# Tanh-gated double matmul on one core: transposing x on the DMA crossbar, 512-column matmuls over mixed w1|w2 banks, and a head run slice by slice

## The chip, the cores and the metric

One NeuronCore of one Trainium2 chip. The metric is the device time of one execution in microseconds, as the median of several runs. The profiler's record of one execution gives the span and the trace that the text reads.

## The reference

```python
# x: (16, 512, 1024) float32; w1, w2: (1024, 768) float32
y1 = np.matmul(x, w1)
y2 = np.matmul(x, w2)
return (np.tanh(y1) * y2).astype(np.float32)
```

## The kernel before

The 16 x 512 rows of x are 64 row tiles of 128 rows (`mt`). The 1024 values of k are 8 slices of 128 (`ko`); the 768 output columns are two halves of 384 (`nt`). Products run on TensorE in bf16 and are summed in float32 in PSUM.

The weights come first: two DMAs on SP's queue (L48, L49) load w1 and w2 whole, 3 MB each, as float32, and one cast each (L52, L53) makes the bf16 copies `w1_b` and `w2_b`. The framework puts the first cast on DVE and the second on ACT, since `nc.any` leaves the engine open.

Then one loop over the 64 row tiles. A DMA on POOL's queue loads a row tile and casts it to bf16 on the way (`x_b`, L63, four buffers). TensorE needs the slice with k on the partitions, so each of the eight 128x128 blocks is transposed by a matmul with an identity into PSUM (`pt`, L67, four banks), and copied to `xT` in SBUF by ACT or DVE (L68). For each half, sixteen matmuls of 384 columns follow, taking turns between the bank of w1 (`ps1`, L77) and the bank of w2 (`ps2`, L79); both have two buffers. ACT takes the tanh of `ps1` into `t1` (L82), DVE multiplies it with `ps2` into `o` (L84), and SP stores the half (L85).

Every matmul is preceded on TensorE by the load of its stationary operand (the 128x128 block of `xT`), which the trace shows as PEld. Each engine works its instructions off in order; the framework's scheduler sets that order and the waits. In `[waits ...]` below, DMASW and DMAHW are completions of DMAs issued from POOL and from SP, eight counters of each in turn, and PE, DVE and Activation are completions on these engines.

Of the kernel before, what the change touches and what calls it, by code (L numbers as in the profile page):

```python
# [1 line left out]

# [5 lines left out]


@with_exitstack
def kernel(
    ctx: ExitStack,
    tc: tile.TileContext,
    x: bass.AP,
    w1: bass.AP,
    w2: bass.AP,
    out: bass.AP,
):
    nc = tc.nc  # L20
    P = 128
    B, M, K = x.shape
    K2, N = w1.shape
    assert K == K2
    BM = B * M
    assert BM % P == 0 and K % P == 0
    KO = K // P
    MT = BM // P
    N_TILE = 384
    assert N % N_TILE == 0  # L30
    NT = N // N_TILE

    xf = x.flatten_outer_dims().rearrange("(mt p) k -> mt p k", p=P)
    of = out.flatten_outer_dims().rearrange("(mt p) n -> mt p n", p=P)
    w1r = w1.rearrange("(ko ki) n -> ki ko n", ki=P)
    w2r = w2.rearrange("(ko ki) n -> ki ko n", ki=P)

    bf16 = mybir.dt.bfloat16
    f32 = mybir.dt.float32

    const = ctx.enter_context(tc.tile_pool(name="const", bufs=1))
    ident = const.tile([P, P], bf16)
    make_identity(nc, ident)

    wpool = ctx.enter_context(tc.tile_pool(name="wpool", bufs=1))
    w1_f = wpool.tile([P, KO, N], f32)
    w2_f = wpool.tile([P, KO, N], f32)
    nc.sync.dma_start(w1_f, w1r)  # L48
    nc.sync.dma_start(w2_f, w2r)  # L49
    w1_b = wpool.tile([P, KO, N], bf16)  # L50
    w2_b = wpool.tile([P, KO, N], bf16)
    nc.any.tensor_copy(w1_b, w1_f)  # L52
    nc.any.tensor_copy(w2_b, w2_f)  # L53

    xpool = ctx.enter_context(tc.tile_pool(name="xpool", bufs=4))
    xtpool = ctx.enter_context(tc.tile_pool(name="xtpool", bufs=4))
    tppool = ctx.enter_context(tc.tile_pool(name="tp_psum", bufs=4, space=bass.MemoryType.PSUM))
    mmpool = ctx.enter_context(tc.tile_pool(name="mm_psum", bufs=2, space=bass.MemoryType.PSUM))
    opool = ctx.enter_context(tc.tile_pool(name="opool", bufs=4))

    for mt in range(MT):
        x_b = xpool.tile([P, K], bf16, tag="x_b")
        nc.gpsimd.dma_start(x_b, xf[mt])  # L63
        xT = xtpool.tile([P, KO, P], bf16)
        for ko in range(KO):
            pt = tppool.tile([P, P], bf16, tag="tp")
            nc.tensor.transpose(pt, x_b[:, ko * P:(ko + 1) * P], ident)  # L67
            nc.any.tensor_copy(xT[:, ko, :], pt)  # L68

        for nt in range(NT):  # L70
            ns = nt * N_TILE
            ps1 = mmpool.tile([P, N_TILE], f32, tag="ps1")
            ps2 = mmpool.tile([P, N_TILE], f32, tag="ps2")
            for ko in range(KO):
                st = ko == 0
                sp = ko == KO - 1
                nc.tensor.matmul(ps1, xT[:, ko, :], w1_b[:, ko, ns:ns + N_TILE],  # L77
                                 start=st, stop=sp)
                nc.tensor.matmul(ps2, xT[:, ko, :], w2_b[:, ko, ns:ns + N_TILE],  # L79
                                 start=st, stop=sp)  # L80
            t1 = opool.tile([P, N_TILE], f32, tag="t1")
            nc.scalar.activation(t1, ps1, mybir.ActivationFunctionType.Tanh)  # L82
            o = opool.tile([P, N_TILE], f32, tag="o")
            nc.vector.tensor_tensor(o, t1, ps2, mybir.AluOpType.mult)  # L84
            nc.sync.dma_start(of[mt, :, ns:ns + N_TILE], o)  # L85


# [1 line left out]
_INS = ['x', 'w1', 'w2']  # L89
_OUTS = [((16, 512, 768), 'float32')]  # L90


# [23 lines left out]
```

## Time and profile before

| | us |
|---|---|
| median of 3 runs | 414.83 |
| lowest, highest | 414.63, 414.93 |
| span of the profiled execution | 413.0 |
| TensorE busy with matmuls in it | 381.2 |
| ACT, DVE, POOL busy | 128.7, 107.2, 36.8 |

The span runs from the first instruction to the last. The time of a run is taken around the execution and is a little longer than the span. The profiled execution has no time of its own outside the profiler, so the median stands beside its span. Busy time of matmuls counts each record to its modelled end, which lies after the start of the next one; what one matmul costs in a stream is therefore read from the step between starts. The page of the profile gives, below the busy times, DMA queues (packets, megabytes, the time that their packets took as a share of the time of 16 engines), the chain of work that ended last, and groups of instructions as `line engine op out<-in xcount | busy, mean ns of one | idle time before them, and who ended it`.

### The profile page before, as it was taken

What the parts mean: (1) busy time and instruction counts of PE and PEld (TensorE: products, weight loads), DVE (VectorE), ACT (ScalarE), POOL (GpSimd) and SP (SyncE); (2) the same over time, 40 slices, a digit from 0 to 9 for tenths busy, and PEclk for the clock granted to TensorE, in tenths of its full rate; (3) what the DMA queues carried; (4) which work ended last, traced back from release to release, by engine and by line L of the source; (5) the groups of instructions that cost most, each with busy time, mean ns of one, the idle gap of its engine ahead of it and who ended that gap; (6) DMA issues with size and microseconds to landing.
All of it is one profiled execution on the core that took longest, in us unless ns stands there. A gap on an engine that the chain in (4) does not pass through costs nothing.

```text
span 413.0 us, 6572 instructions
## 1 busy us (share of the span) xinstructions
PE 381.2 (92%) x2560; PEld 235.9 (57%) x2560; DVE 107.2 (26%) x316; ACT 128.7 (31%) x455; POOL 36.8 (9%) x70
## 2 busy tenths in 40 slices
PE   1496999999999999999999999999999999999995
PEld 0253666666666666666666666666666666666663
DVE  0301232232223232222323232232223232222322
ACT  1434132332333233323323332332333233323322
POOL 2400001110110011011101101110110011011000
PEclk9998999999999999999999999999999999999999
DMA  8971345444444543444354345434444543444221
GB/s 255 294 264 40 101 123 119 107 108 116 110 109 101 129 109 104 110 108 117 95 128 108 106 106 120 111 102 116 109 110 102 128 106 106 108 110 116 71 77 58
DMA packets 29760, 48.67 MB, mean 118 GB/s; under 512 B 3104, under 2 KB 19488, under 8 KB 29728
## 3 DMA queue, kind: packets, MB, share of 16 engines
q0 software_dynamic: 9216, 16.78, 24.7%
q1 hardware_dynamic: 20512, 31.47, 21.1%
q8 instruction: 20, 0.33, 0.3%
q14 instruction: 12, 0.10, 0.1%
HBM read 39.85 MB, written 25.17 MB: 157 GB/s over the span
## 4 chain that ended last, share of the span: by engine, by line
PE 86%; DMA 7%; DVE 3%; ACT 1%; issue 1%; SPq 0%
PE ps L79 41%; PE ps L77 38%; PE pt L67 7%; DMA w_f<-in_w_dram 7%; DVE xT L68 3%; ACT w_b L53 1%; DVE o L84 0%; ACT t L82 0%; SPq L48 0%
## 5 line engine op out<-in xcount | busy, mean ns | idle before, releaser
L79 PE MATMUL ps<-w_b,xT 128*128 128x384 bf16 x1024 | 326.7, 328 | 4.2 <-ACT w_b L53 4.2
L77 PE MATMUL ps<-w_b,xT 128*128 128x384 bf16 x1024 | 327.0, 328 | 1.6 <-DVE w_b L52 1.6
L82 ACT ACTIVATE t<-ps 128x384 f32<-128x384 f32 x128 | 62.7, 490 | 266.8 <-PE ps L77 263.3
L77 PEld LDWEIGHTS <-xT 128*128 128x128 bf16 x1024 | 100.6, 98 | 77.4 <-issue 19.7
L79 PEld LDWEIGHTS <-xT 128*128 128x128 bf16 x1024 | 100.5, 98 | 67.9 <-issue 6.0
L84 DVE TENSOR_TENSOR o<-t,ps 128x384 f32<-128x384 f32 x128 | 70.9, 554 | 179.7 <-ACT t L82 158.5
L67 PE MATMUL pt<-ident,x_b 128*128 128x128 bf16 x512 | 64.0, 223 | 21.5 <-DMA x_b<-in_x_dram 12.5
L68 ACT COPY xT<-pt 128x128 bf16<-128x128 bf16 x325 | 65.6, 271 | 11.7 <-PE pt L67 11.1
L63 POOL DMA_DIRECT2D x_b<-in_x_dram x64 | 36.2, 566 | 342.9 <-PE pt L67 342.5
L68 DVE COPY xT<-pt 128x128 bf16<-128x128 bf16 x187 | 36.0, 221 | 117.5 <-PE pt L67 114.7
L67 PEld LDWEIGHTS <-x_b 128*128 128x128 bf16 x512 | 39.7, 99 | 26.9 <-DMA x_b<-in_x_dram 13.9
L53 ACT CAST w_b<-w_f 128x6144 bf16<-128x6144 f32 x1 | 5.3, 5312 | 1.0 <-DMA w_f<-in_w_dram 1.0
L52 DVE CAST w_b<-w_f 128x6144 bf16<-128x6144 f32 x1 | 3.4, 3361 | 5.1 <-DMA w_f<-in_w_dram 5.1
L68 ACT ACT_TABLE_LOAD x1 | 1.3, 1283 | 0.7 <-PEq L100 0.7
masks.py:199 POOL TENSOR_SCALAR_AFFINE_SELECT ident<-ident 128x128 bf16<-128x128 bf16 x1 | 0.3, 304 | 0.1
masks.py:197 POOL MEMSET ident<- 128x128 bf16 x1 | 0.2, 204 | 0.3 <-POOLq L100 0.3
L100 POOL MEMSET const-float32-0.0<- 128x1 f32 x1 | 0.1, 98 | 0.2 <-issue 0.2
L100 POOL MEMSET const-bfloat16-1.0<- 128x1 bf16 x1 | 0.1, 102 | 0.0
L100 POOL MEMSET const-uint8-127<- 128x1 uint8 x1 | 0.1, 102 | 0.0
L100 POOL MEMSET const-float32-1.0<- 128x1 f32 x1 | 0.1, 98 | 0.0
## 6 DMA issues: line engine op xcount, KB each, us to landing
out_dram<-o SPq DMA_DIRECT2D x128, 192.0 KB, 1.9
x_b<-in_x_dram POOLq DMA_DIRECT2D x64, 256.0 KB, 3.7
w_f<-in_w_dram SPq DMA_DIRECT2D x2, 3072.0 KB, 22.0
```

What stands on the lines that cost most here:

```text
L52: nc.any.tensor_copy(w1_b, w1_f)
L53: nc.any.tensor_copy(w2_b, w2_f)
L63: nc.gpsimd.dma_start(x_b, xf[mt])
L67: nc.tensor.transpose(pt, x_b[:, ko * P:(ko + 1) * P], ident)
L68: nc.any.tensor_copy(xT[:, ko, :], pt)
L77: nc.tensor.matmul(ps1, xT[:, ko, :], w1_b[:, ko, ns:ns + N_TILE], start=st, stop=sp)
L79: nc.tensor.matmul(ps2, xT[:, ko, :], w2_b[:, ko, ns:ns + N_TILE], start=st, stop=sp)
L82: nc.scalar.activation(t1, ps1, mybir.ActivationFunctionType.Tanh)
L84: nc.vector.tensor_tensor(o, t1, ps2, mybir.AluOpType.mult)
L100: nc = _bacc.Bacc("TRN2", target_bir_lowering=False, num_devices=1)
```

## The change

- x is still loaded and cast by POOL's queue (`load_x`), into eight buffers. A DMA on SP's queue, `dma_start_transpose`, then writes `xT` from `x_b`, in SBUF, in place of eight transposes on TensorE and eight copies. The identity is gone.
- The weights are no longer loaded whole and cast by an engine. POOL's queue loads them with cast in slices of one k each (`load_w`), into eight tiles `w_b[k]` that hold, for each of three chunks of 256 columns, 256 of w1 beside 256 of w2. The slices of the first two chunks come first, with the loads of the first four row tiles between them, then the slices of the third chunk.
- One matmul covers a whole chunk: 512 columns, w1 and w2 in one PSUM bank (`mm`). All eight banks are one ring (`bank`). The tanh reads the left half of a bank, the product the right half (`finish`), 256 columns each. A row tile is stored by one DMA of 768 columns (`store`).
- The first four row tiles are run with k as the outer loop over their first two chunks, in eight banks; their third chunk follows, row tile by row tile. From the fifth row tile on, the loop runs row tile by row tile, three chunks of eight matmuls each, with `load_x` called four row tiles ahead.
- `pin` keeps every instruction in the order of the code on its engine.

```diff
-    w1_f = wpool.tile([P, KO, N], f32)
-    w2_f = wpool.tile([P, KO, N], f32)
-    nc.sync.dma_start(w1_f, w1r)
-    nc.sync.dma_start(w2_f, w2r)
-    nc.any.tensor_copy(w1_b, w1_f)
-    nc.any.tensor_copy(w2_b, w2_f)
-        for ko in range(KO):
-            pt = tppool.tile([P, P], bf16, tag="tp")
-            nc.tensor.transpose(pt, x_b[:, ko * P:(ko + 1) * P], ident)
-            nc.any.tensor_copy(xT[:, ko, :], pt)
...
+    HALF = 256
+    NC = N // HALF
+    HEAD = 4
+    AHEAD = 4
...
+    xpool = ctx.enter_context(tc.tile_pool(name="xpool", bufs=HEAD + AHEAD))
+    xtpool = ctx.enter_context(tc.tile_pool(name="xtpool", bufs=HEAD + AHEAD))
+    pspool = ctx.enter_context(tc.tile_pool(name="ps", bufs=8, space=bass.MemoryType.PSUM))
+    tpool = ctx.enter_context(tc.tile_pool(name="tpool", bufs=4))
     opool = ctx.enter_context(tc.tile_pool(name="opool", bufs=4))
+    w_b = [wpool.tile([P, NC, 2, HALF], bf16, name=f"w_b{k}") for k in range(KO)]
+    def load_w(k, c0, c1):
+        for h, src in ((0, w1r), (1, w2r)):
+            pin(nc.gpsimd.dma_start(
+                w_b[k][:, c0:c1, h, :],
+                src[:, k, c0 * HALF:c1 * HALF].rearrange("p (c j) -> p c j", j=HALF)))
+    def load_x(mt):
+        x_b = xpool.tile([P, K], bf16, tag="x_b", name="x_b")
+        pin(nc.gpsimd.dma_start(x_b, xf[mt]))
+        xT = xtpool.tile([P, KO, P], bf16, tag="xT", name="xT")
+        pin(nc.sync.dma_start_transpose(xT, x_b))
+        xts[mt] = xT
+    def finish(mt, c, ps, o):
+        t1 = tpool.tile([P, HALF], f32, tag="t1", name="t1")
+        pin(nc.scalar.activation(t1, ps[:, :HALF], ACT.Tanh))
+        pin(nc.vector.tensor_tensor(o[:, c * HALF:(c + 1) * HALF], t1, ps[:, HALF:], ALU.mult))
+    def mm(ps, mt, k, c):
+        pin(nc.tensor.matmul(ps, xts[mt][:, k, :], w_b[k][:, c, :, :].rearrange("p h j -> p (h j)"),
+                             start=k == 0, stop=k == KO - 1))
...
+    for k in range(3, KO):
+        load_w(k, 0, 2)
+    for k in range(KO):
+        load_w(k, 2, NC)
+    for mt in range(HEAD, HEAD + AHEAD):
+        load_x(mt)
+    head = {(mt, c): bank() for mt in range(HEAD) for c in range(2)}
+    for k in range(KO):
+        for mt in range(HEAD):
+            for c in range(2):
+                mm(head[mt, c], mt, k, c)
...
+    for mt in range(HEAD, MT):
+        if mt + AHEAD < MT:
+            load_x(mt + AHEAD)
+        o = new_o()
+        for c in range(NC):
+            ps = bank()
+            for k in range(KO):
+                mm(ps, mt, k, c)
+            finish(mt, c, ps, o)
+        store(mt, o)
```

The order of instructions at three places. First POOL, from the start of the program, before: the loads of x alone, with the identity between them.

```order
masks.py:197 MEMSET ident 128x128
L63 DMA x_b<-in_x_dram 128x1024
masks.py:199 ISA
masks.py:199 AFFINE_SELECT ident<-ident 128x128
L63 DMA x_b<-in_x_dram 128x1024 x63
```

POOL after, from its first DMA; the slices of two chunks are `128x2x256`.

```order
L63 DMA x_b<-in_x_dram 128x1024
L57 DMA w_b_73<-in_w_dram 128x2x256 x2
L63 DMA x_b<-in_x_dram 128x1024
L57 DMA w_b_74<-in_w_dram 128x2x256 x2
L63 DMA x_b<-in_x_dram 128x1024
L57 DMA w_b_75<-in_w_dram 128x2x256 x2
L63 DMA x_b<-in_x_dram 128x1024
L57 DMA w_b_76<-in_w_dram 128x2x256 x2
```

The weights have moved from SP's queue to POOL's, and the fourth row tile's load stands behind six weight slices. Sixteen slices of the first part, sixteen of the second and sixty loads of x make up the rest of the row.

Second, SP's queue, before, with waits: the weights, then one store after another, each waiting for DVE.

```order
L48 DMA w_f<-in_w_dram 128x8x768
L49 DMA w_f<-in_w_dram 128x8x768
L85 DMA out_dram<-o 128x384 [waits DVE_49] x6
L85 DMA out_dram<-o 128x384 [waits DMAHW0_49,DVE_49]
L85 DMA out_dram<-o 128x384 [waits DMAHW1_49,DVE_49]
```

SP's queue after, from the transposes of the seventh and eighth row tile to the tenth's.

```order
L65 DMA_TRANSPOSE xT<-x_b 128x8x128 [waits DMASW6_49]
L65 DMA_TRANSPOSE xT<-x_b 128x8x128 [waits DMASW7_49]
L77 DMA out_dram<-o 128x768 [waits DMAHW0_49,DVE_49]
L77 DMA out_dram<-o 128x768 [waits DMAHW1_49,DVE_49]
L77 DMA out_dram<-o 128x768 [waits DMAHW2_49,DVE_49]
L77 DMA out_dram<-o 128x768 [waits DMAHW3_49,DVE_49]
L65 DMA_TRANSPOSE xT<-x_b 128x8x128 [waits DMAHW4_49,DMASW0_49,PE_49]
L77 DMA out_dram<-o 128x768 [waits DMAHW5_49,DVE_49]
L65 DMA_TRANSPOSE xT<-x_b 128x8x128 [waits DMAHW6_49,DMASW1_49,PE_49]
```

Transposes and stores now share the queue: a transpose waits for its x_b, and every store stands behind the transpose ahead of it and the other way round.

Third, TensorE after, from its first matmul, which waits for the first weight slice (DMASW1); the numbers are those of buffers.

```order
L80 MATMUL ps_145<-w_b0_73,xT_83 128x512 [waits DMASW1_49]
L80 LDWEIGHTS xT_83
L80 MATMUL ps_146<-w_b0_73,xT_83 128x512
L80 LDWEIGHTS xT_89 [waits DMAHW1_49]
L80 MATMUL ps_147<-w_b0_73,xT_89 128x512
L80 LDWEIGHTS xT_89
L80 MATMUL ps_148<-w_b0_73,xT_89 128x512
L80 LDWEIGHTS xT_95 [waits DMAHW2_49]
L80 MATMUL ps_149<-w_b0_73,xT_95 128x512
L80 LDWEIGHTS xT_95
L80 MATMUL ps_150<-w_b0_73,xT_95 128x512
L80 LDWEIGHTS xT_101 [waits DMAHW3_49]
```

The first slice of k is run for all four row tiles before the second slice, so the fourth row tile's transpose (DMAHW3) stands ahead of all that follows. Before, TensorE's first work was the transposes of the row tiles that had been loaded, and its first product waited for the cast of a whole weight.

More of the change, by code (lines that the diff above doesn't have):

```diff
@@ L5 @@
 import concourse.tile as tile
-from concourse import bass_utils, mybir
+from concourse import mybir
 from concourse._compat import with_exitstack
-from concourse.masks import make_identity
+ACT = mybir.ActivationFunctionType
+ALU = mybir.AluOpType
 @with_exitstack
@@ L22 @@
     B, M, K = x.shape
-    K2, N = w1.shape
-    assert K == K2
+    _, N = w1.shape
     BM = B * M
-    assert BM % P == 0 and K % P == 0
     KO = K // P
     MT = BM // P
-    N_TILE = 384
-    assert N % N_TILE == 0
-    NT = N // N_TILE
+    HALF = 256
+    NC = N // HALF
+    HEAD = 4
+    AHEAD = 4
+    bf16 = mybir.dt.bfloat16
+    f32 = mybir.dt.float32
     xf = x.flatten_outer_dims().rearrange("(mt p) k -> mt p k", p=P)
@@ L36 @@
     w2r = w2.rearrange("(ko ki) n -> ki ko n", ki=P)
[L38 to L43, printed above, removed]
-    wpool = ctx.enter_context(tc.tile_pool(name="wpool", bufs=1))
-    w1_f = wpool.tile([P, KO, N], f32)
-    w2_f = wpool.tile([P, KO, N], f32)
-    nc.sync.dma_start(w1_f, w1r)
-    nc.sync.dma_start(w2_f, w2r)
-    w1_b = wpool.tile([P, KO, N], bf16)
@@ L51 @@
[L51 to L58, printed above, removed]
-    opool = ctx.enter_context(tc.tile_pool(name="opool", bufs=4))
@@ L61 @@
[L61 to L64, printed above, removed]
-        for ko in range(KO):
-            pt = tppool.tile([P, P], bf16, tag="tp")
[L67 to L85, printed above, removed]
@@ new lines, in finish, with new_o, store @@
+    def finish(mt, c, ps, o):
+        t1 = tpool.tile([P, HALF], f32, tag="t1", name="t1")
+        pin(nc.scalar.activation(t1, ps[:, :HALF], ACT.Tanh))
+        pin(nc.vector.tensor_tensor(o[:, c * HALF:(c + 1) * HALF], t1, ps[:, HALF:], ALU.mult))
+    def new_o():
+        return opool.tile([P, N], f32, tag="o", name="o")
+    def store(mt, o):
+        pin(nc.sync.dma_start(of[mt], o))
+    def mm(ps, mt, k, c):
+        pin(nc.tensor.matmul(ps, xts[mt][:, k, :], w_b[k][:, c, :, :].rearrange("p h j -> p (h j)"),
+                             start=k == 0, stop=k == KO - 1))
@@ new lines, in bank @@
+    def bank():
+        return pspool.tile([P, 2 * HALF], f32, tag="ps", name="ps")
+    load_x(0)
+    load_w(0, 0, 2)
+    load_x(1)
+    load_w(1, 0, 2)
+    load_x(2)
+    load_w(2, 0, 2)
+    load_x(3)
+    for k in range(3, KO):
[9 more added lines that the diff above has]
+                mm(head[mt, c], mt, k, c)
@@ new lines @@
+    outs = [new_o() for _ in range(HEAD)]
+    for mt in range(HEAD):
+        for c in range(2):
+            finish(mt, c, head[mt, c], outs[mt])
+    for mt in range(HEAD):
+        ps = bank()
+        for k in range(KO):
+            mm(ps, mt, k, 2)
+        finish(mt, 2, ps, outs[mt])
+        store(mt, outs[mt])
+    for mt in range(HEAD, MT):
[3 more added lines that the diff above has]
+        for c in range(NC):
+            ps = bank()
+            for k in range(KO):
+                mm(ps, mt, k, c)
+            finish(mt, c, ps, o)
+        store(mt, o)
```

2 lines of the change are left out of this document (added).

## The prediction

> **What bounds the kernel now.** First the head of the page and the chain of waits, to see which engine carries the end; then the timeline of the first 44 us and of one row tile in the middle; last the queues and groups, for prices.
>
> ```profile
> span 413.0 us, 6572 instructions
> PE 381.2 (92%) x2560; PEld 235.9 (57%) x2560; DVE 107.2 (26%) x316; ACT 128.7 (31%) x455; POOL 36.8 (9%) x70
> by line: PE ps L79 40.7%; PE ps L77 38.4%; PE pt L67 7.1%; DMA w_f<-in_w_dram 6.7%; DVE xT L68 3.4%; ACT w_b L53 1.3%; issue 1.0%; DVE o L84 0.1%; ACT t L82 0.1%; SPq L48 0.1%
> 1.24 27.87 DMA w_f<-in_w_dram
> 29.13 5.32 ACT w_b L53
> 34.49 9.64 PE ps L79 x48
> ```
>
> TensorE, busy 92%, carries the end. The chain has two parts that are not product: the transposes with the copies behind them (7.1% + 3.4% of 413.0 = 43.4 us), and a head of 34.5 us in which w2 is loaded whole and cast whole.
>
> ```profile
> 20.31 9.92 PE L77 MATMUL ps<-w_b,xT 128*128 128x384 bf16 x48 [1.64 <-DVE w_b L52]
> 103.68 0.32 PE L77 MATMUL ps<-w_b,xT 128*128 128x384 bf16 x1
> ...
> 108.39 0.33 PE L79 MATMUL ps<-w_b,xT 128*128 128x384 bf16 x1
> 108.55 0.75 PE L67 MATMUL pt<-ident,x_b 128*128 128x128 bf16 x5
> 403.25 0.21 PE pt L67 x3
> 34.50:44.00 9.50, 9.50 (x49) 5.29 (x49) 2.77 (x5) 1.66 (x6) 0.00 (x0) 0.82 0.23 85
> 120.00:240.00 120.00, 117.05 (x803) 73.06 (x801) 32.72 (x100) 37.82 (x140) 10.55 (x20) 1.00 0.46 111
> ```
>
> In the head only 48 of the 2048 matmuls run before 34.49. In the middle, 103.68 to 108.39 are 29 steps of one 384-column matmul: 4.71 / 29 = 0.1624 us each. The last column but two of the windows is the granted clock: 1.00 in the middle, 0.82 from 34.5 to 44, just after TensorE stood still. The next figure, 0.46, is the share of the DMA engines.
>
> **The matmuls.** 2048 of 384 columns become 64 x 3 x 8 = 1536 of 512, the same columns in all. The price of 512 isn't in the trace. In proportion to columns it is 0.1624 x 512/384 = 0.2166 us. The three 128-column transposes (0.21 us, 0.07 each) give the other end: a straight line from 0.07 at 128 through 0.1624 at 384 reaches 0.2086. I take 0.2166, since 384 is nearer to 512 and the transposes are another kind of matmul. The other end is 1530 x 0.008 = 12 us less. (The Trainium skill, TensorE: Matmul & The Clock Gate, Part 1, gives 215.7 ns from start to start for 512 columns at full clock; the sum by it is 1.4 us lower.) The weight load of each (98 ns, below) fits under 0.2166, as it did under 0.1624. The mixed w1|w2 bank costs TensorE nothing: the operand is still 512 columns in a row.
>
> **Transposes, copies, casts and identity: removed.** Of ACT's and DVE's copies only the 3.4% in the chain was path; the rest lay beside matmuls. Tanh and product go from 2 x 384 to 3 x 256 columns.
>
> ```profile
> L82 ACT ACTIVATE t<-ps 128x384 f32<-128x384 f32 x128 | 62.7, 490 | 266.8 <-PE ps L77 263.3
> L79 PEld LDWEIGHTS <-xT 128*128 128x128 bf16 x1024 | 100.5, 98 | 67.9 <-issue 6.0
> L84 DVE TENSOR_TENSOR o<-t,ps 128x384 f32<-128x384 f32 x128 | 70.9, 554 | 179.7 <-ACT t L82 158.5
> L63 POOL DMA_DIRECT2D x_b<-in_x_dram x64 | 36.2, 566 | 342.9 <-PE pt L67 342.5
> ```
>
> A 256-column tanh lies between 327 ns (in proportion) and 490, a product between 369 and 554. Even at the upper ends a row tile asks 3 x 0.49 = 1.5 us of ACT and 1.7 of DVE in its 24 x 0.2166 = 5.20 us, with eight banks in the ring: hidden.
>
> **The crossbar.** Each row tile issues one more DMA, on SP, in front of a store.
>
> ```profile
> q0 software_dynamic: 9216, 16.78, 24.7%
> q1 hardware_dynamic: 20512, 31.47, 21.1%
> HBM read 39.85 MB, written 25.17 MB: 157 GB/s over the span
> out_dram<-o SPq DMA_DIRECT2D x128, 192.0 KB, 1.9
> x_b<-in_x_dram POOLq DMA_DIRECT2D x64, 256.0 KB, 3.7
> L85 SPq DMA_DIRECT2D out_dram<-o x128: 332/332/360, 37.9 to 409.5; - x128
> ```
>
> One load of x takes 0.247 x 413.0 / 64 = 1.59 us of all 16 engines. The hardware queue takes 0.211 x 413.0 = 87.1 us for 31.47 MB, of which 25.17 is output: 69.7 us, 1.09 per row tile. Together 2.68 of the coming 5.20, so a transpose may take 2.5 us of the engines before they fill. No crossbar row exists. Its 256 KB at the rate of the hardware queue (44 ps per byte per engine) are 0.73 us. If instead each of its 1024 pieces of 256 B costs a whole packet of that queue (87.1 x 16 / 20512 = 68 ns), it is 4.35 us. I take 0.73: packets here are paid by the byte. Of the HBM read, 33.55 MB is x as float32, so a load's packet moves 33.55 MB / 9216 = 3.6 KB, 2.4 times the 1.5 KB of the hardware queue's, and costs 0.247 x 413.0 x 16 / 9216 = 177 ns, 2.6 times. Both ends stay for the range. SP's issue isn't shown either: a store's 0.33, or, were each of the eight blocks issued by itself, 2.7, which with the store still fits 5.20; I take 0.33. Latency: 0.33 to issue, 1.9 to land as a store does, 0.73: 3.0 us from x_b to xT. In the steady part a row tile is transposed about four tiles, 20 us, ahead of its use, and POOL runs ahead of SP, so 3 us is covered. The store queued behind a transpose waits at most that long; four output buffers give it 20 us. If the transpose outgrew 2.5 us that cover would drain, tile by tile, and xT would be what TensorE waits for.
>
> **The head.** Whole loads and casts give way to 32 slice loads with cast on POOL's queue, with x between them.
>
> ```profile
> 1.27 0.66 POOL L63 DMA_DIRECT2D x_b<-in_x_dram  x1 [0.32 <-issue]
> 2.26 1.62 POOL L63 DMA_DIRECT2D x_b<-in_x_dram  x3
> 17.62 2.76 POOL L63 DMA_DIRECT2D x_b<-in_x_dram  x1 [1.87 <-PE pt L67]
> L63 POOL DMA_DIRECT2D x_b<-in_x_dram x64: 527/527/2760, 1.3 to 379.8; - x64
> 408.17 0.33 PE L79 MATMUL ps<-w_b,xT 128*128 128x384 bf16 x1
> 409.47 0.33 SPq L85 DMA_DIRECT2D out_dram<-o  x1
> ```
>
> A load of x is 128 runs and 0.53 us of POOL. A first-part slice (two chunks) is 256 runs: between 0.53 and twice that, 1.05, which I take; a second-part slice is 128 runs, 0.53. With the identity gone POOL starts at about 0.9. Ahead of x3 stand three loads of x and six slices: 0.9 + 1.6 + 6.3 = 8.8; landed 3.7 later, 12.5 (by the engines' time, 4 x 1.59 + 6 x 0.80 = 11.2 us of loads, it could be 1 to 2 us later); transposed 15.5. TensorE starts at 0.9 + 3.7 + 3.0 = 7.6 with tile 0 but, in order, can't pass the fourth tile's first slice before 15.5, having done 6 matmuls. The last first-part slice is issued by 9.3 + 10 x 1.05 = 19.8 and lands at 23.5, ahead of its use near 28. From 15.5 come 58 matmuls (12.6) and a cold start: the two stretches of 48 matmuls took 9.92 and 9.64 where 48 x 0.1624 = 7.8, so 1.8 to 2.1 lost; 2.0 here. That is 30.1. The second-part slices are issued by 28.3 and land by 32.0; the first row tile needs the last of them at 31.6, a stall of 0.4. Its bank is free: the first of the eight is finished 7 matmuls (1.5 us) before the last, and tanh plus product take 1.05 at most. The 32 matmuls end at 37.4; x4 is issued at 28.3, landed at 32.0, transposed at 35.0, in time.
>
> **The sum.** 15.5 to pass x3, 2.0 cold, 1530 x 0.2166 = 331.4, stall 0.4, and the end: last matmul done at 408.3 of 413.0, so 4.7 from there through tanh, product and store (the smaller tanh and product save at most 0.35, the larger store gives that back). Together 354.0 of span. The runs' median, 414.83, stands 1.83 over the profiled span: 355.8, so 356.
>
> **Rivals.**
>
> (a) The crossbar becomes the bound, the one that ends slower. At 4.35 us per row tile the DMA engines need 1.59 + 1.09 + 4.35 = 7.03, against 5.20 on TensorE. Head 37.4, 8.7 later since four transposes of 4.35 stand in line before x3 is through (4.6 + 2.2 + 17.4 = 24.2), 60 x 7.03 = 422, end 4.7: 473 of span, 475. At 177 ns a piece it is 11.3 us, and beyond 850. It decides from 37.4 + 60t + 4.7 = 413, t = 6.18, a transpose of 3.5 us, or 55 ns a piece. For it: nothing in the trace moves pieces this small, and all 1024 must pass. Against: packets here cost by bytes, 11 ns for 256 B. The Trainium skill speaks for it in VectorE: DVE Perf Modes, The three transpose paths: 1309 ns for a 128x128 block by the crossbar against 390 on TensorE; eight in a row would be 10.5 us, an estimate from that page, and more than 680 us in all. Its DMA: Bandwidth & Descriptors, Latency and other measured facts, has 261 GB/s, 1.0 us. No run here shows either yet. Chance 0.14.
>
> (b) Transposes crawl only while loads are queued. If each of an engine's 64 pieces waits for a load's packet of 177 ns, a transpose takes 12 us until the loads end near 32. Tile 0 is ready at 18.6, tile 1 near 31, the fourth at 34 in place of 15.5: 18.5 later, 374. For it: the windows' engines were 0.96 busy in the first 20 us below. Against: engines drain several pieces at a turn if these are joined. Chance 0.10.
>
> ```profile
> 0.00:20.00 20.00, 5.92 (x35) 3.38 (x36) 4.52 (x9) 5.84 (x25) 6.89 (x14) 1.00 0.96 274
> ```
>
> (c) POOL's issuing sets the head. One load took 2.76 us of POOL while DVE's cast ran beside it; no such cast is left, but at 2.1 us a first-part slice the 16 end 16.8 later, the last second-part slice lands at 48.8, and the four head tiles end at 54.2, not 37.4: 373. Chance 0.06.
>
> (d) The change doesn't do what it says: a transpose between 2.5 and 3.5 us gives the removed 43 us back as a wait for xT, 356 to 415. Chance 0.04, one quarter of it within 0.2% or above.
>
> **How the numbers follow.** My forecast, all transposes covered, has 0.66; its own range is 347 (three quarters of the 12 us of the 0.2086 end) to 364 (x3 later by 2, SP's issue of 2.7 in the head, a second cold start, 2 more). The range asked reaches over (b) and (c), to 382: 0.66 + 0.10 + 0.06 = 0.82. Slower is (a): 0.14 and a little of (d). 0.2%, 0.8 us, is about what a measurement of this kernel can tell from no change; 0.01 for that. Faster is the rest, 0.84.
>
> **What would show it.** Right: a 512-column step of 0.215 to 0.217 us; TensorE with no wait for xT after 40 us; the engines' share near (2.68 + 0.73) / 5.20 = 0.66; the fourth tile's first matmul near 15.5; the fifth tile near 37; last matmul 4.7 before the end. Wrong: DMA xT as the releaser of matmuls, tile after tile, with a DMA share of 0.9 (a); the same in the first 35 us alone (b); POOL busy without a gap to 45 us with matmuls waiting for w_b (c).

## The result: faster, by 13 us less than the sum said

| | before | after |
|---|---|---|
| median of the runs, us | 414.88 | 368.81 |
| lowest, highest | 414.63, 415.94 | 367.95, 370.02 |
| ratio, 95% interval | | 0.890, 0.887 to 0.893 |
| profiled span, us | 413.0 | 368.3 |

The forecast was 356, its range 347 to 382. The profiled execution is the longest of the four, 370.02 us, so its span lies 1.2 us higher than one of the median would. The page of the kernel after, its head, queues and chain by line:

```profile
span 368.3 us, 4126 instructions
PE 334.8 (91%) x1506; PEld 150.7 (41%) x1536; DVE 80.0 (22%) x192; ACT 74.1 (20%) x193; POOL 54.0 (15%) x100
q1 hardware_dynamic: 76800, 41.96, 51.6%
q0 software_dynamic: 15872, 19.93, 39.8%
PE ps L80 90%; DMA xT<-x_b 3%; DMA x_b<-in_x_dram 3%; POOL w_b L57 1%; POOL x_b L63 0%; DVE o L71 0%; ACT t L70 0%; POOLq L142 0%
```

TensorE is 90% of the chain, now all product. What is left is the head, and the chain in order of time shows it, with the products behind it:

```profile
7.14 11.44 DMA x_b<-in_x_dram
18.59 12.23 DMA xT<-x_b
30.87 12.30 PE ps L80 x43
...
43.23 10.74 PE ps L80 x49
...
54.02 10.74 PE ps L80 x49
...
356.19 7.95 PE ps L80 x36
```

The pieces of 10.74 start 10.79 apart for 50 matmuls (a record is missing in each): 0.2158 us for 512 columns. Before 30.87 stands one load of x, 11.44, and one transpose, 12.23. TensorE's timeline up to there:

```profile
17.36 1.03 PE L80 MATMUL ps<-w_b,xT 128*128 128x512 bf16 x2 [17.36 <-DMA xT<-x_b]
...
23.46 1.03 PE L80 MATMUL ps<-w_b,xT 128*128 128x512 bf16 x2 [5.07 <-DMA xT<-x_b]
...
26.88 1.03 PE L80 MATMUL ps<-w_b,xT 128*128 128x512 bf16 x2 [2.39 <-DMA xT<-x_b]
```

Each of the first four row tiles waits for its xT, and TensorE has done 6 matmuls by 30.87. From there it does not wait for xT again. The forecast's terms against what the profile has:

| term, us | forecast | measured |
|---|---|---|
| past the fourth row tile's xT | 15.5 | 30.87 |
| cold start (12.30 less 43 x 0.2158) | 2.0 | 3.0 |
| 1530 matmuls | 331.4 | 330.2 |
| wait for slices of the third chunk | 0.4 | 0 |
| last matmul to the end | 4.7 | 4.2 |
| span | 354.0 | 368.3 |

So one term is off by 15.4 and the others by about 1 or less. How long a transpose takes from issue to landing, for three stretches of this trace (the source line's view; the line names L65 gives the time of its issue on SP): the head, the middle, and the end, where no load of x is left.

```profile
L65 SPq DMA_TRANSPOSE xT<-x_b x4: 1535/3002/3842, 4.9 to 18.6; - x4
DMA to landing us min/median/max: 11.1/12.3/14.3
...
L65 SPq DMA_TRANSPOSE xT<-x_b x47: 1283/1305/4176, 60.8 to 298.4; - x47
DMA to landing us min/median/max: 3.4/5.4/9.1
...
L65 SPq DMA_TRANSPOSE xT<-x_b x6: 1282/1300/2701, 313.7 to 339.6; - x6
DMA to landing us min/median/max: 3.4/3.4/5.0
```

The sum had 3.0 everywhere. That is nearly right for the quiet end (3.4), and four times too little in the head. A landing is counted from the issue, so it holds the time in line behind an earlier transpose too; the second to the fourth xT come 6.1, 3.4 and 4.0 after the one before.

### The profile page after: what moved, and what is told of

It is laid out like the page before. It is cut to its first block, busy times and chain, and to the rows that moved or that the text cites. A ratio compares the mean times of both kernels' runs of the same rounds, so it can differ in the third digit from the quotient of the medians.

```text
span 368.3 us, 4126 instructions
## 1 busy us (share of the span) xinstructions
PE 334.8 (91%) x1506; PEld 150.7 (41%) x1536; DVE 80.0 (22%) x192; ACT 74.1 (20%) x193; POOL 54.0 (15%) x100
## 4 chain that ended last, share of the span: by engine, by line
PE 90%; DMA 6%; POOL 2%; issue 1%; DVE 0%; ACT 0%; POOLq 0%
PE ps L80 90%; DMA xT<-x_b 3%; DMA x_b<-in_x_dram 3%; POOL w_b L57 1%; POOL x_b L63 0%; DVE o L71 0%; ACT t L70 0%; POOLq L142 0%
## 5 line engine op out<-in xcount | busy, mean ns | idle before, releaser
L80 PE MATMUL ps<-w_b,xT 128*128 128x512 bf16 x1506 | 334.8, 382 | 29.3 <-DMA xT<-x_b 27.8
L80 PEld LDWEIGHTS <-xT 128*128 128x128 bf16 x1536 | 150.7, 98 | 212.9 <-DMA xT<-x_b 30.5
L71 DVE TENSOR_TENSOR o<-t,ps 128x256 f32<-128x256 f32 x192 | 80.0, 421 | 285.0 <-ACT t L70 280.8
L70 ACT ACTIVATE t<-ps 128x256 f32<-128x256 f32 x192 | 72.8, 384 | 289.7 <-PE ps L80 280.3
L63 POOL DMA_DIRECT2D x_b<-in_x_dram x64 | 34.3, 548 | 238.9 <-DMA xT<-x_b 237.8
L57 POOL DMA_DIRECT2D w_b<-in_w_dram x32 | 19.8, 636 | 12.6 <-DMA w_b<-in_w_dram 7.5
```

The source lines that it names most:

```text
L57: pin(nc.gpsimd.dma_start(w_b[k][:, c0:c1, h, :], src[:, k, c0 * HALF:c1 * HALF].rearrange("p (c j) -> p c j", j=HALF)))
L63: pin(nc.gpsimd.dma_start(x_b, xf[mt]))
L70: pin(nc.scalar.activation(t1, ps[:, :HALF], ACT.Tanh))
L71: pin(nc.vector.tensor_tensor(o[:, c * HALF:(c + 1) * HALF], t1, ps[:, HALF:], ALU.mult))
L80: pin(nc.tensor.matmul(ps, xts[mt][:, k, :], w_b[k][:, c, :, :].rearrange("p h j -> p (h j)"), start=k == 0, stop=k == KO - 1))
```

## The experiments

The theory after the result, A: a transpose is slow where loads stand queued, since its 256-byte pieces take turns with the loads' packets on the DMA engines. Rivals: B, the first transposes are slow in themselves; C, the fourth row tile's load, behind six slices, is what comes late.

**No weight packet beside the first four transposes.** A copy on POOL that reads the fourth xT holds the weights back.

```diff
-    load_x(0)
-    load_w(0, 0, 2)
...
+    for mt in range(HEAD):
+        load_x(mt)
+    gate = tpool.tile([P, 1], bf16, tag="gate", name="gate")
+    pin(nc.gpsimd.tensor_copy(gate, xts[HEAD - 1][:, 0, 0:1]))
+    for k in range(KO):
+        load_w(k, 0, 2)
```

> The changed kernel, but the four first loads of x come first on POOL's queue, and a small copy on POOL that reads the fourth row tile's xT stands ahead of all weight loads, so no weight packet shares the DMA engines with the first four transposes. Theory A (a transpose's pieces take turns with load packets on each engine; alone it takes about 3.4 us, as the last six of the steady part do): the four transposes are through by 13 to 16 us instead of 30.9; the weights then start late, and the four head tiles end near 37 to 39; time 353 to 357. Theory B (the first transposes are slow in themselves and stand in line, whatever else is queued): the fourth is through at 28 to 31 us as now, the weights come after it, and the time is 370 or more.

370.33 us. The transposes' landing and the copy that waited for the fourth, then TensorE, in this run:

```profile
L65 SPq DMA_TRANSPOSE xT<-x_b x4: 1302/1339/3947, 5.1 to 11.8; - x4
DMA to landing us min/median/max: 3.2/4.7/6.5
...
15.02 0.19 POOL L91 COPY gate<-xT 128x1 bf16<-128x1 bf16 x1 [11.54 <-DMA xT<-x_b]
...
19.57 17.53 PE L80 MATMUL ps<-w_b,xT 128*128 128x512 bf16 x71 [19.57 <-DMA w_b<-in_w_dram]
...
38.91 5.57 PE L80 MATMUL ps<-w_b,xT 128*128 128x512 bf16 x25 [1.81 <-DMA w_b<-in_w_dram]
...
51.99 10.25 PE L80 MATMUL ps<-w_b,xT 128*128 128x512 bf16 x34 [7.51 <-DMA xT<-x_b]
```

The fourth is through at 15.0 instead of 30.9, each in 3.2 to 6.5 us. B falls: the first transposes of a program aren't slow in themselves. The packets of the two queues while the four are moved, in the kernel after from 9.1 to 30.3 us, then in this run from 8.5 to 14.5:

```profile
q0 software_dynamic: 4237, 2.41, 88.7%
q1 hardware_dynamic: 4224, 1.05, 47.8%
...
q1 hardware_dynamic: 4224, 1.05, 105.3%
q0 software_dynamic: 59, 0.08, 7.8%
```

The same 4224 packets of the crossbar (q1) take 21 us beside 4237 packets of loads, and 6 us beside 59.

The time that A gave was missed by 13 all the same. The weights start only behind the gate, so the first product comes at 19.57 and the head ends at 44.5 instead of 37 to 39. And the last row shows a second wait: the fifth row tile's transpose runs beside eight loads of x that POOL lets go together once the weights are out; it is issued at 40.5 and holds TensorE for 7.51 until 51.99. The slow transposes had only moved to the next burst of loads.

**Loads of x first, weights at once behind them.**

```diff
-    load_x(0)
-    load_w(0, 0, 2)
...
+    for mt in range(HEAD):
+        load_x(mt)
+    for k in range(KO):
+        load_w(k, 0, 2)
```

> The changed kernel, with the first four loads of x ahead of all weight slices on POOL's queue. Theory A (turns with load packets): the weight slices are still queued beside the transposes, which stay 6 to 12 us each in line; the fourth is through at 27 to 31 us; time 365 to 369. Rival C (the fourth row tile is late because its load stood behind six slices and landed at 18.6 instead of 12.5): its load lands by 11, the fourth transpose is through near 22, time 358 to 361.

366.43 us. The four transposes, and the products behind the fourth:

```profile
L65 SPq DMA_TRANSPOSE xT<-x_b x4: 2787/3882/4039, 4.8 to 15.5; - x4
DMA to landing us min/median/max: 10.5/12.2/12.5
...
28.00 34.30 PE L80 MATMUL ps<-w_b,xT 128*128 128x512 bf16 x149 [3.00 <-DMA xT<-x_b]
```

Here the loads of x land within 7.6 us of issue, so C falls: a fourth load some 8 us earlier brings its xT only 2.9 earlier. Beside the weight slices the transposes stay slow, and the fourth waits for the line of three in front of it more than for its load.

**The first four row tiles transposed on TensorE.** Eight blocks into one bank, one copy on DVE.

```diff
-        pin(nc.sync.dma_start_transpose(xT, x_b))
+        if mt < NPE:
+            xbs[mt] = x_b
+        else:
+            pin(nc.sync.dma_start_transpose(xT, x_b))
...
+    def turn(mt):
+        pt = pspool.tile([P, KO, P], bf16, tag="ps", name="pt")
+        for k in range(KO):
+            pin(nc.tensor.transpose(pt[:, k, :], xbs[mt][:, k * P:(k + 1) * P], ident))
+        pin(nc.vector.tensor_copy(xts[mt], pt))
```

> The changed kernel, with the first four row tiles transposed on TensorE (eight blocks into one PSUM bank, one copy of 1024 columns on DVE) instead of by the crossbar; the other sixty as in the changed kernel. Theory A: x3 is in SBUF by 12 to 14 us and its products start by 15; TensorE then goes at the pace of the weight slices; the fifth row tile's transpose comes after most loads. Span 351 to 356, time 353 to 358. Rival C (the load of x3 itself is what is late): x3 lands at 18.6 as now, products from 20, time 358 to 361. Theory B gains as A does here unless the fifth row tile's transpose, now the first, takes 12 us by itself and holds TensorE: 360 to 364.

362.11 us. TensorE and SP in this run:

```profile
16.17 22.72 PE L94 MATMUL ps<-w_b,xT 128*128 128x512 bf16 x96
...
32.86 11.54 SPq L73 DMA_TRANSPOSE xT<-x_b  x4
43.31 18.91 PE L94 MATMUL ps<-w_b,xT 128*128 128x512 bf16 x79 [4.42 <-DMA xT<-x_b]
```

The head's products end at 38.9, some 14 us sooner (30.87 + 3.0 + 90 x 0.2158 = 53.3 in the kernel after), and then the fifth row tile's transpose, issued at 32.86 beside a burst of loads, holds TensorE for 4.42. The time lies in the band given for B, but the run above had ruled B out; it is the burst again, and A's own number had left it out.

**The first eight on TensorE, loads of x first.** The same with `NPE = 8` and the order of the second experiment; the fifth to the eighth are transposed one row tile ahead of use.

> As the run with four row tiles transposed on TensorE, but the first eight are (the fifth to the eighth one row tile ahead of use, among the products), and the first four loads of x come first on POOL's queue. The first crossbar transpose is then that of the ninth row tile, which is needed near 53 us. Theory A (transposes crawl only while loads stand queued): nothing waits for xT; products start near 10, the third chunks of the head end near 33, eight blocks four times cost 2 to 3 us of TensorE; span 349 to 353, time 351 to 355. Rival D (the weight slices set the pace of the head): waits for w_b appear in the first 30 us, time 356 to 360.

353.86 us, ratio to the kernel before 0.853 (0.851 to 0.854). No product waits for an xT of the crossbar. These are all the waits of products, and in the chain the products are one piece from 50.09 on:

```profile
PE ps L94 <- DVE xT L80: 0.8, 1, 0.8
PE ps L94 <- DMA w_b<-in_w_dram: 0.4, 1, 0.4
...
50.09 298.73 PE ps L94 x1384
```

The ninth row tile's transpose, issued at 38.6, still takes 10.2 us to land, but is needed much later. Against the kernel after it is 15.0 us less, about the 15.4 by which the term of the head was off; up to 2.4 of it may be the order of the loads, which differed by that much alone. Of rival D little is seen: TensorE waits twice for a weight slice, 0.4 with a product and 0.6 with the load of a stationary operand, and the chain up to 29.68 runs over POOL's issuing of slices, but its 356 to 360 isn't reached.

**The crossbar alone.** The kernel before with one line in place of transposes and copies.

```diff
-        for ko in range(KO):
-            pt = tppool.tile([P, P], bf16, tag="tp")
-            nc.tensor.transpose(pt, x_b[:, ko * P:(ko + 1) * P], ident)
-            nc.any.tensor_copy(xT[:, ko, :], pt)
+        nc.sync.dma_start_transpose(xT, x_b)
```

> The kernel before with one part of the change alone: the crossbar transpose on SP's queue in place of the transposes on TensorE and the copies; weights whole, 384 columns, two banks as before. If the transposes and copies on the chain (43.4 us) are simply gone: 413.0 - 43.4 + 1.8 = 371, which would leave 2 us for all the rest of the change. Rival by theory A: the first transposes stand behind 6 MB of weight packets on SP's own queue, land only after 28 us, and the 48 products that ran before 34.5 us come after it: 376 to 384.

365.99 us: this one line gives a little more than the whole change (0.8%; the intervals of the ratios, 0.880 to 0.885 and 0.887 to 0.893, don't meet). The end of its head:

```profile
24.03 5.31 ACT L53 CAST w_b<-w_f 128x6144 bf16<-128x6144 f32 x1 [2.52 <-DMA w_f<-in_w_dram]
24.99 5.09 PE L74 MATMUL ps<-w_b,xT 128*128 128x384 bf16 x16 [24.99 <-DMA xT<-x_b]
29.91 2.76 PE L76 MATMUL ps<-w_b,xT 128*128 128x384 bf16 x16
```

Both expectations are missed. The first transpose lands at 24.99, 16.4 us after its issue, where the rival said after 28. It is late for another reason than turns: it stands behind the weights on SP's own queue, and up to 23.1 the trace has no packet of its size. The framework has also put both casts on ACT, which takes up the second as soon as w2 is there. And w2, which landed at 29.1 before, lands at 24.0; four loads of x were issued before that where there had been eight, which is the likely reason and not tested. So products of w2 start at 29.91 instead of 34.49, which makes up what the rival had counted as lost and 5 us of the 371. The kernel after stands at 30.87 with less done.

**The change without the crossbar.** `NPE = MT`: every row tile transposed on TensorE, one row tile ahead.

> The changed kernel with every row tile transposed on TensorE (eight blocks into one bank, one DVE copy of 1024 columns, one row tile ahead of use): the change without the crossbar. If a block costs 0.07 us of TensorE, a row tile costs 0.56 more: 39 for the head, 60 x (5.18 + 0.56) = 344 and 4.2 to the end, 388 of span, 389 to 392 in time. Rival: with one copy in place of eight and no wait of TensorE for it, the blocks slip in at less, 380; or the whole bank's copy holds TensorE and the price of before (0.71) stays, 398.

383.30 us. Two row tiles in the chain:

```profile
41.27 5.18 PE ps L94 x24
46.90 5.18 PE ps L94 x24
```

They start 5.63 apart, so eight blocks cost 0.45 here, where the kernel before had 0.80 over its 32 x 0.1624; less than either price that I gave. The form with one copy of 1024 columns is not in the change, so 383.3 is the best case of the rest of it.

This run saves 31.5 us, the crossbar alone 48.8, the whole change 46.0. The first two overlap: 60 x (0.80 - 0.45) = 21 of the 31.5 are cheaper transposes, which the crossbar run saves as well. By this estimate the head and the wide matmuls are worth some 10 without the crossbar, and 48.8 + 10 would be 59. The 13 that are missing are near what the slow transposes cost in the head: there the crossbar runs beside the slices.

**Each transpose twice.**

```diff
+        if mt >= 2 * HEAD:
+            dump = dpool.tile([P, KO, P], bf16, tag="dump", name="dump")
+            pin(nc.sync.dma_start_transpose(dump, x_b))
```

> The changed kernel with each row tile from the ninth on transposed twice on SP's queue, the second time into a buffer that nothing reads: the steady part's room for the crossbar. By the packet records at their median (18 ns a 256-byte piece, 172 a load packet, 122 a store packet) a row tile asks 2 x 1.15 + 1.38 + 0.98 = 4.7 us of the engines, under 5.18: TensorE still doesn't wait, 368 to 371. By their mean (27, 243, 137 ns) it asks 2 x 1.7 + 1.9 + 1.1 = 6.4: the engines become the bound and 56 row tiles are 1.2 us longer, 430 to 445.

367.87 us, no slower. The chain, and the last two figures of the window (share of the DMA engines, GB/s):

```profile
29.54 331.99 PE ps L84 x1530
...
100.00:200.00 100.00, 100.00 (x465) 45.37 (x464) 24.34 (x58) 22.21 (x58) 10.04 (x19) 1.00 1.13 227
```

1530 matmuls without a wait, beside two transposes in every 5.18 us. In the kernel after the share in the same stretch is 0.93 with one. It passes 1 here, so it can't be the share of time in which the engines are occupied: records of packets overlap. Of the two prices in the expectation, the median's was the one that held.

**Packets of 2 KB.** The loads of x first, and a weight tile that keeps w1 and w2 as whole rows, so that the slices of the first part move in half as many packets.

```diff
-    w_b = [wpool.tile([P, NC, 2, HALF], bf16, name=f"w_b{k}") for k in range(KO)]
+    w_b = [wpool.tile([P, 2, N], bf16, name=f"w_b{k}") for k in range(KO)]
...
-                w_b[k][:, c0:c1, h, :],
-                src[:, k, c0 * HALF:c1 * HALF].rearrange("p (c j) -> p c j", j=HALF)))
+                w_b[k][:, h, c0 * HALF:c1 * HALF],
+                src[:, k, c0 * HALF:c1 * HALF]))
```

> As the run with the four loads of x first, but a weight tile keeps w1 and w2 each as a whole row, so a first-part slice moves 128 runs of 2 KB instead of 256 of 1 KB; the same bytes in half as many packets, the matmul reading its 512 columns in two pieces of 256. Theory A in its sharp form (each 256-byte piece waits for one load packet): where the transposes follow one another at 4.0 to 4.4 us beside 1 KB packets, they follow at 6 to 7 us beside 2 KB packets; the fourth is through at 32 to 36 us in place of 28.0; time 370 to 375. Rival E (the engines are shared by bytes, so packet size is nothing): spacing stays 4.0 to 4.4, the fourth by 28, time 365 to 368.

367.52 us. TensorE's first four starts:

```profile
16.98 1.03 PE L80 MATMUL ps<-w_b,xT 128*128 128x512 bf16 x2 [16.98 <-DMA xT<-x_b]
24.48 1.03 PE L80 MATMUL ps<-w_b,xT 128*128 128x512 bf16 x2 [6.46 <-DMA xT<-x_b]
27.01 1.03 PE L80 MATMUL ps<-w_b,xT 128*128 128x512 bf16 x2 [1.50 <-DMA xT<-x_b]
28.95 16.31 PE L80 MATMUL ps<-w_b,xT 128*128 128x512 bf16 x67 [0.90 <-DMA xT<-x_b]
```

The first spacing is 7.5 in place of 4.4, as A's sharp form asks; the next two are 2.5 and 1.9, after the 2 KB packets were out, and the fourth is through at 28.95, a microsecond past E's band, and the time lies within it. Both expectations fail in a part. The counts of packets from 10 to 22 us say more, first with 1 KB packets (the second experiment), then with 2 KB:

```profile
q0 software_dynamic: 2892, 1.40, 87.5%
q1 hardware_dynamic: 2884, 0.72, 50.2%
...
q0 software_dynamic: 1918, 1.74, 89.6%
q1 hardware_dynamic: 2099, 0.52, 35.0%
```

In both runs the crossbar moves about one packet for each packet of the loads, and with 2 KB packets a quarter fewer in the same time. So the turns of A are borne out, and E, by which the size is nothing, is not. A's times failed because the larger packets are through sooner, and the last two transposes then go faster.

**Both together.** The fastest kernel with that weight layout.

> The fastest so far (eight row tiles transposed on TensorE, loads of x first) with the same weight layout: 128 runs of 2 KB a first-part slice, 0.53 us of POOL instead of 0.70. No crossbar transpose runs beside the weights, so theory A has nothing to slow; POOL is through the slices 3 us sooner. If POOL's issuing held the third chunks: 351 to 353. Rival: TensorE's own work and its cold start set the head, 353 to 355; or the moving operand in two pieces costs TensorE something per matmul, 1536 x 5 ns and more, above 360.

353.71 us (ratio 0.852, 0.849 to 0.855), the same as 353.86. POOL's faster issuing is worth nothing there, and a moving operand in two pieces costs nothing that can be measured.

## Why the prediction was right, and the step that was off

- **The range** holds the measured time by its reach, not by the account behind 356. That account had its own range, 347 to 364, and 368.8 lies above it; up to 382 the range had been stretched for rivals (b) and (c).
- **The steady part** came out as worked out: step 0.2158 (forecast 0.2166; the 215.7 ns of the Trainium skill's page TensorE: Matmul & The Clock Gate, Part 1, agree), no wait for xT after 30.87, tanh 384 and product 421 ns hidden, 4.2 us to the end. Main mechanism, transposes off TensorE's chain: shown by the crossbar-alone run.
- **The step that failed** is the head's "transposed 15.5": landing 12.5 plus 3.0. The load landed at 18.6 and the transpose took 12.2 more. The 3.0 was a price for quiet engines, put into a stretch whose engines the prediction itself quoted as 0.96 busy, and it was counted once where four transposes stand in line. That line, not the late load, set the 30.87: with the load 8 us earlier it was 28.00, and with the weights held back 15.0.
- **Rival (b)**, transposes that crawl while loads are queued, is what happened (forecast of its time 374, of the first tile 18.6, of the second 31, of the fourth 34; measured 368.8, 17.4, 23.5, 30.9). It had 0.10. Its mechanism is right and its price too high: at 177 ns a piece each transpose would take about 12 us, and the last three came 3.4 to 6.1 apart. That the first came close, 12.4 us after its issue, is in part luck, since a transpose needs 3.4 of that on quiet engines too.
- **Rival (a)** is out. A transpose's packets take (0.516 x 368.3 - 69.7) / 64 = 1.88 us by the queue's share if the stores still take 69.7 (an estimate), between my ends of 0.73 and 4.35; but the room I had put at 2.5 us is larger: two per row tile fit. The 1309 ns a block of the Trainium skill's page VectorE: DVE Perf Modes, The three transpose paths, can't be taken as a rate: sixteen blocks in 5.18 us are 0.32 each at most. The 261 GB/s of the Trainium skill's page DMA: Bandwidth & Descriptors, Latency and other measured facts, isn't contradicted: in the gated run the crossbar, alone on the engines from 10.8 to 14.5 us, moved 213 GB/s on average.
- **Rival (c)** is out: a slice of 256 runs took 0.70 to 0.78 us of POOL where I took 1.05. SP's issue of a transpose, taken as 0.33, is 1.3, up to 6.0; the steady part covers it.
- **The share of the engines**, forecast 0.66, is 0.93 to 0.97. As the doubled run shows, that sum can't be read as a limit.
- **Slices against whole loads**: the forecast lies 15 us under the 371 that the crossbar alone would have left, so it gave the head and the wide matmuls 15. They are worth some 10 without the crossbar, by the estimate above, and -2.8 with it (365.99 against 368.81).

## What to carry to other kernels

Price a DMA that other work waits for by the stretch it runs in: the same transpose took 3.4 us on quiet engines and 11 to 14 behind a burst of loads, and where it is in the head that wait is paid in full. Use the crossbar where it has several tiles' lead, and TensorE, idle anyway, for the tiles that open the program; of the kernels run here that split, with eight tiles, is the fastest, by 12 us over the crossbar alone. Try the parts of a change singly: one line of this one saved 49 us, the whole 46.

## What the hardware showed that I had not expected

The DMA engines' share passed 1 (1.13 over 100 us) with TensorE still never waiting: the records of packets overlap. A piece of 256 bytes on the crossbar goes with about one packet of a load, of 1 KB or of 2. And a burst of loads slows whatever transposes follow it: wherever the weights were moved, the next transpose in line took 10 to 12 us (fifth row tile 11.4 and 10.4, ninth 10.2).
